# A two-layer hybrid decoder trunk: a recurrence without reciprocals, an output projection prepared in steps, value products of a pair in one go, and a compressed branch on the whole array

## The chip, the core and the metric

The kernel runs on one core of one Trainium2 chip. The time is what the device takes for one execution, in microseconds (us). Five engines have a part in it, each with its own instruction queue: TensorE (PE, with its weight loads PEld), VectorE (DVE), ScalarE (ACT), GpSimd (POOL) and SyncE (SP), which only starts transfers here. [...]

## The reference

Input is `x` (1024 rows of width 1024) and a memory of 256 rows. There are two layers. Each normalizes, projects once, runs three token mixers side by side, multiplies each with its own SiLU gate, and projects the joined result back with a residual sum.

Layer 0 mixes by sliding-window attention (A, 8 heads, window 128), by a gated linear recurrence (B, width 512), and by attention into the memory (M, 4 heads):

```python
# B, the recurrence
r = sigmoid(xh @ w_r + b_r); i = sigmoid(xh @ w_i + b_i)
log_a = -B_C * r * softplus(-lam)
a = exp(log_a)
u = sqrt(-expm1(2.0 * log_a)) * (i * xc)
h_t = a_t * h_(t-1) + u_t
...
return h + concatenate([oa, ob, om]) @ w_out
```

Layer 1 mixes by a chunked gated recurrence (C), by sparse attention (D, 8 heads in 2 groups) and again by attention into the memory. D has three branches, each with its own gate: a compressed one, which attends to 63 compressed keys of 64 numbers a group; a selected one, which attends to the chosen blocks; and a window of 512:

```python
p_c = softmax(where(mask_c, q @ kc * scale, NEG_INF))   # 63 compressed keys
o_cmp = p_c @ vc
...
o = g[..., 0, :] * o_cmp + g[..., 1, :] * o_sel + g[..., 2, :] * o_win
```

## The kernel before, in words

Projections are made of three matmuls each, of a high and a low part in place of f32 (`mm3`, L393 to L398): high by high, high by low, low by high. Scores are two such matmuls (L476, L477). Transposes (L256) and value products (L1436, L666, L813, L1364) are plain f32, of which a transpose is one instruction on PE and a product two.

The program is traced as generators. A main one goes through attention tiles of 128 rows; `weave` adds side generators to it. A side is written as (generator, n, y0, y1): its n steps are spread over the main steps y0 to y1. The order of each engine's queue comes from a scheduler at compile time, which takes the traced order as priority, holds each named ring of tiles to its count (the `B_` constants: `B_TR` for the transpose banks `tr`, `B_PT` for the transposed probabilities `PT`, `B_PS` for the probability tiles `Pt`, `B_HW` for the half-width tiles), and lets an instruction that is ready go ahead of one that isn't. Each engine then runs its queue in that order.

**Layer 0** has 24 tiles (8 of each attention group, then 8 of the memory attention) in a pipeline of 52 main steps: project, turn, probabilities, values. Beside them runs `side`, 24 steps from main step 0 to `E0`: gates and four blocks of the recurrence (`rglru_block`, L872), each in two halves of 128 x 512. A half makes a convolution on DVE (L890), two matmuls with tanh (L895, L896), a third tanh (L897), a square root (L899), a reciprocal (L902), products on POOL (L903, L904), the scan (L907) and the product with the gate (L508), and is stored to DRAM by `keep` (L540).

The output projection of layer 0 for rows 0 to 511 is `out_proj`, 16 steps from main step `E1` to `E2`. Its inputs are ten pieces of 128 x 512: eight come back from DRAM (`mixin`, L1469), two are the memory attention's, still in SBUF. `mix_parts` splits each into a high part on ACT (L1472) and a low part on DVE (L1473). A load must wait for a marker, `self.near`: a one-element copy on POOL (L1468) from a query tile of the memory attention, written where `s % 4 == NR` (L633). Called without a list `hl`, `out_proj` runs all of `mix_parts` in its first step. With a list it uses what another side has made; layer 1 did so already (L959).

**Layer 1** runs `nsa` twice, once a group, 8 tiles each. A tile has eight units, two for each pair: the window branch (`b` = 1) and the selected branch (`b` = 0), each with two pairs of heads. The first unit of a pair scores one head (`scored(0)`); `front` scores the other, takes the exponents (L1412) and scales (L1416). What is left of a pair is put on a list `late`, from which each unit takes one item as soon as more than two are on it. Before, a pair leaves two items, the first and the second half of its key tiles, in twos: each item transposes its tiles (`turned`, a copy out of PSUM by ACT, L1428) and multiplies them (`times`, L1436), where two heads fill the two halves of the array's columns. All branches of a tile add up in the one bank `ov`. `coarse` (L1353) begins that sum with the compressed branch: four transposes of 128 x 63, one copy (L1362), and two products of 64 columns by 256 (L1364).

Of the kernel before, what the change touches and what calls it, by code (L numbers as in the profile page):

```python
# [5 lines left out]
F32 = mybir.dt.float32  # L6
# [3 lines left out]
AF = mybir.ActivationFunctionType  # L10
# [4 lines left out]
P = 128  # L15
# [35 lines left out]
E0 = 38  # L51
# [13 lines left out]
B_TR = 4  # L65
B_OV = 1
NV = 4
N_LC0 = 1274
N_LC1 = 2428
B_PC = 3  # L70
N_FIX = 2966
NR = 2
# [9 lines left out]
def weave(main, *sides):  # L82
    drain(woven(main, *sides))
# [66 lines left out]
class Trunk:  # L150
# [108 lines left out]
    def setup(self):  # L259
        nc, I, const = self.nc, self.I, self.fixed  # L260
        self.ident = const.tile([P, P], F32, name="ident")
        nc.sync.dma_start(self.ident, I["c_ident"])
        rows = self.gt("rows", [P])
        for i, x in enumerate(("mem_norm_g", "norm_g")):
            nc.sync.dma_start(rows[16 * i:16 * i + 16, :], I[x].rearrange("l (k p) -> (l k) p", p=P))
        pt = self.tr()
        self.transpose(pt[:, 0, 0:32], rows[0:32, :], 32)
        self.gains = const.tile([P, 32], F32, name="gains")
        nc.vector.tensor_copy(self.gains, pt[:, 0, 0:32])
        self.mhalf = const.tile([P, 1], F32, name="mhalf")  # L270
# [235 lines left out]
    def mixmul(self, dst, o):  # L506

        self.nc.vector.scalar_tensor_tensor(out=dst, in0=o, scalar=0.5, in1=dst, op0=ALU.mult, op1=ALU.mult)  # L508
# [177 lines left out]
    def layer0(self):  # L686
# [73 lines left out]
        weave(pipe(tiles), (self.side, 24, 0, E0), (self.out_proj(0, I["ev_w_out"][0], 0, I["x"][0], self.h1), 16, E1, E2))  # L760
# [61 lines left out]
    def rglru_setup(self):  # L822
# [32 lines left out]
        nc.vector.scalar_tensor_tensor(out=sp2, in0=acc, scalar=4.0, in1=nl, op0=ALU.mult, op1=ALU.add)  # L855
        tiny = self.lc.tile([P, 1], F32, name="tiny")
# [7 lines left out]
        return prm, hb, sp2, tiny, bd  # L864
# [7 lines left out]
    def rglru_block(self, blk, b, prm, hb, sp2, tiny, bd, m):  # L872
# [3 lines left out]
        for half in range(2):  # L876
# [16 lines left out]
            for i, dst in enumerate((tr_, ti)):  # L893
                ps = self.sc()
                nc.tensor.matmul(ps, bd[:, i, b, :], xc, start=True, stop=True)  # L895
                nc.scalar.activation(dst, ps, AF.Tanh, scale=0.5, bias=hb[:, 4 * i + b:4 * i + b + 1])  # L896
            nc.scalar.activation(tr_, tr_, AF.Tanh, scale=sp2[:, b:b + 1], bias=sp2[:, b:b + 1])  # L897
            nc.vector.scalar_tensor_tensor(out=ti, in0=ti, scalar=1.0, in1=xc, op0=ALU.add, op1=ALU.mult)
            nc.scalar.activation(xc, tr_, AF.Sqrt, bias=tiny)  # L899
            nc.vector.tensor_scalar(out=tr_, in0=tr_, scalar1=1.0, scalar2=None, op0=ALU.add)  # L900
            inv = self.hw("inv", [H])
            nc.vector.reciprocal(inv, tr_)  # L902
            nc.gpsimd.tensor_tensor(out=xc, in0=xc, in1=inv, op=ALU.mult)  # L903
            nc.gpsimd.tensor_tensor(out=ti, in0=ti, in1=xc, op=ALU.mult)  # L904
            nc.vector.tensor_scalar(out=inv, in0=inv, scalar1=2.0, scalar2=-1.0, op0=ALU.mult, op1=ALU.add)
# [5 lines left out]
            self.mixmul(m[:, half, :], tr_)  # L911
# [300 lines left out]
    def compress(self, w):  # L1212
# [6 lines left out]
        vc = lc.tile([64, 2, HD], F32, name="vc")  # L1219
        kcT = lc.tile([P, 2, 64], F32, name="kcT")  # L1220
        self.cmp = (kcT, vc)
        for kind in range(2):
# [36 lines left out]
            hid = self.w1("hid", [2, 64])  # L1259
# [8 lines left out]
            nc.vector.scalar_tensor_tensor(out=hid[:, :, :NC], in0=th, scalar=1.0, in1=z, op0=ALU.add, op1=ALU.mult)  # L1268
            zc = self.sc()[0:NC, 0:P].rearrange("p (g d) -> p g d", g=2)
            for g in range(2):  # L1270
                nc.tensor.matmul(zc[:, g, :], hid[:, g, :NC], w2, start=True, stop=True)
            if kind == 1:
                nc.vector.tensor_copy(vc[0:NC], zc)
                yield
                continue
            n3 = lambda name: self.w1(name, [2, HD])[0:NC]
# [21 lines left out]
    def nsa_tile(self, blk, s, g, mixD):  # L1298
# [54 lines left out]
        def coarse():  # L1353
# [4 lines left out]
            pt = self.tr()  # L1358
            for h in range(4):
                self.transpose(pt[0:NC, h, :], pc[:, h, :NC])  # L1360
            PT = self.w2("PT", [4, P])
            nc.scalar.copy(PT[0:NC], pt[0:NC])  # L1362
            for f in range(2):
                nc.tensor.matmul(ov[f * HD:(f + 1) * HD, :], vc[0:NC, g, :], PT[0:NC].rearrange("p (h f) q -> p f h q", f=2)[:, f],  # L1364
                                 start=True, stop=False)

        def pair(b, hp):
# [72 lines left out]
            cut = (len(q0s) + 1) // 2  # L1440

            def back(part):
                for q0 in part:
                    turned(q0)
                for q0 in part:
                    times(q0)
                if part is q1 and b == 0 and hp == 1:
                    self.finish(1, 4 + 4 * g, s, mixD, st["ov"])

            q1 = q0s[cut:]  # L1450
            return [(lambda: scored(0), []), (front, [lambda: back(q0s[:cut]), lambda: back(q1)])]
# [126 lines left out]
```

## Time and profile before

| | |
|---|---|
| median of 3 runs | 1484.0 us (1481.54 to 1485.84) |
| the profiled execution: time, span | 1481.0 us, 1479.2 us |
| PE busy, instructions | 1406.0 us (95%), 10051 |
| DVE, ACT, POOL busy | 865.2, 657.6, 709.6 us |
| mean granted clock of PE | 0.982 |
| transfers | 108.54 MB, mean 73 GB/s |

Busy time is the share of the span in which an engine has at least one instruction under way; since matmuls are pipelined, a mean time of one matmul is longer than the distance to the next, so the text takes starts. The first projection of layer 1 follows the last output projection of layer 0 at 547 us. In rows of groups the columns are line, engine, operation, output from inputs, shapes and count, then busy time and mean ns of one, then the engine's idle time just before them and what ended it.

### The profile page before, as it was taken

How to read it: one execution, taken by the hardware profiler on the slowest of the kernel's cores; microseconds unless marked ns; L12 is line 12 of the kernel's file. 1: busy time of each engine (PE TensorE's matmuls, PEld its weight loads, DVE VectorE, ACT ScalarE, POOL GpSimd, SP SyncE). 2: the span in 40 equal slices, each digit the busy share in tenths (PEclk: the TensorE clock that was granted, in tenths of full speed). 3: DMA queues.
4: the chain of work that ended last, by engine and by line, in shares of the span. 5: the costliest groups of instructions: out<-in, count | busy, mean ns of one | idle time of the engine just before them, and what ended most of it. 6: DMA issues, size and time to landing. Idle time of an engine off the chain costs nothing.

```text
span 1479.2 us, 27613 instructions
## 1 busy us (share of the span) xinstructions
PE 1406.0 (95%) x10051; PEld 1222.1 (83%) x10051; DVE 865.2 (58%) x2497; ACT 657.6 (44%) x1636; POOL 709.6 (48%) x1125
## 2 busy tenths in 40 slices
PE   7999999999599999999999999999999988899999
PEld 6888888788489989898777777799988876788898
DVE  6667986866873428325565565445684567555621
ACT  7545654545553424124444454423342345455531
POOL 6344675564753334126544544335673557354521
PEclk9999999999899999999999999999999999899999
DMA  9420121122355554310000100031121001223323
GB/s 291 129 65 1 58 72 43 42 66 72 99 166 178 183 155 115 98 32 16 15 23 25 56 1 22 16 86 29 30 65 30 8 17 63 81 76 108 115 63 125
DMA packets 120619, 108.54 MB, mean 73 GB/s; under 512 B 19194, under 2 KB 108835, under 8 KB 120483
## 3 DMA queue, kind: packets, MB, share of 16 engines
q1 hardware_dynamic: 119906, 104.68, 23.6%
q0 software_dynamic: 576, 2.10, 0.5%
q8 instruction: 79, 1.29, 0.4%
q14 instruction: 58, 0.47, 0.1%
HBM read 87.35 MB, written 18.35 MB: 71 GB/s over the span
## 4 chain that ended last, share of the span: by engine, by line
PE 80%; DVE 8%; POOL 4%; ACT 3%; issue 3%; DMA 2%; SPq 1%; ACTq 0%; DVEq 0%; POOLq 0%
PE pj L396 17%; PE pj L397 17%; PE pj L398 17%; PE tr L256 8%; PE ov L1436 5%; PE sc L476 3%; PE sc L477 3%; DVE Pt L480 2%; PE sc L1067 1%; PE ov L813 1%; PE ov L666 1%; PE sc L398 1%; DMA mixin<-mix 1%; PE sc L396 1%; PE sc L397 1%
## 5 line engine op out<-in xcount | busy, mean ns | idle before, releaser
L398 PE MATMUL pj<-xn,whl 128*128 128x512 f32 x520 | 206.5, 397 | 0.0
L396 PE MATMUL pj<-xn,whl 128*128 128x512 f32 x520 | 206.3, 397 | 0.0
L397 PE MATMUL pj<-xn,whl 128*128 128x512 f32 x520 | 206.0, 396 | 0.0
L396 PE MATMUL pj<-whl,xn 128*128 128x256 f32 (+1 forms) x680 | 197.0, 293 | 3.6 <-ACT whl L247 3.0
L247 ACT CAST whl<-raw 128x512 fp32r<-128x512 f32 (+1 forms) x212 | 127.6, 614 | 162.6 <-PE pj L398 96.8
L397 PE MATMUL pj<-whl,xn 128*128 128x256 f32 (+1 forms) x680 | 197.4, 291 | 0.3 <-POOL whl L253 0.3
L398 PE MATMUL pj<-whl,xn 128*128 128x256 f32 (+1 forms) x680 | 196.3, 290 | 0.0
L396 PE MATMUL pj<-whl,mhi 128*128 128x256 f32 x640 | 184.1, 290 | 9.8 <-ACT mhi L1472 6.9
L253 POOL TENSOR_TENSOR whl<-raw,whl 128x512 fp32r<-128x512 f32 (+1 forms) x99 | 130.6, 1320 | 124.7 <-ACT whl L247 118.0
L397 PE MATMUL pj<-whl,mhi 128*128 128x256 f32 x640 | 182.8, 288 | 0.0
L398 PE MATMUL pj<-whl,mlo 128*128 128x256 f32 x640 | 179.8, 287 | 0.0
L1416 POOL TENSOR_SCALAR Pt<-Pt,fixed,lc 128x640 f32<-128x640 f32 (+7 forms) x128 | 107.0, 846 | 88.6 <-DVE fixed L1413 72.6
L396 PEld LDWEIGHTS pj<-whl,xn 128*128 128x128 f32 x680 | 129.9, 192 | 8.7 <-ACT whl L247 3.5
L397 PEld LDWEIGHTS pj<-whl,xn 128*128 128x128 f32 x680 | 131.0, 193 | 4.1 <-issue 1.9
L396 PEld LDWEIGHTS pj<-whl,mhi 128*128 128x128 f32 x640 | 123.3, 193 | 12.8 <-ACT mhi L1472 7.8
L253 DVE TENSOR_TENSOR whl<-raw,whl 128x512 fp32r<-128x512 f32 (+1 forms) x113 | 93.7, 832 | 68.0 <-ACT whl L247 67.7
L398 PEld LDWEIGHTS pj<-whl,xn 128*128 128x128 f32 x680 | 130.8, 193 | 1.7 <-issue 1.4
L256 PE MATMUL tr<-fixed,Pt 128*128 128x128 f32 x776 | 127.2, 286 | 5.3 <-DVE fixed L480 0.9
L1428 ACT COPY PT<-tr 128x512 f32<-128x512 f32 (+1 forms) x152 | 75.5, 530 | 114.1 <-PE tr L256 113.2
L1412 ACT ACTIVATE Pt<-Pt,fixed 128x640 f32<-128x640 f32 (+7 forms) x128 | 99.0, 776 | 60.0 <-DVE fixed L1409 32.3
L397 PEld LDWEIGHTS pj<-whl,mhi 128*128 128x128 f32 x640 | 123.9, 194 | 1.3 <-issue 1.2
L398 PEld LDWEIGHTS pj<-whl,mlo 128*128 128x128 f32 x640 | 122.2, 193 | 1.5 <-issue 1.4
(309 smaller groups left out, 3287.7 us busy)
## 6 DMA issues: line engine op xcount, KB each, us to landing
raw<-od_w_in SPq DMA_DIRECT2D x60, 256.0 KB, 3.9
raw<-ev_w_in SPq DMA_DIRECT2D x44, 256.0 KB, 4.4
raw<-ev_w_out SPq DMA_DIRECT2D x40, 256.0 KB, 4.0
raw<-od_w_out SPq DMA_DIRECT2D x40, 256.0 KB, 3.9
mixin<-mix SPq DMA_DIRECT2D x32, 256.0 KB, 3.6
raw<-mem_w_kv SPq DMA_DIRECT2D x16, 256.0 KB, 4.7
x<-x SPq DMA_DIRECT2D x8, 512.0 KB, 6.5
mix<-mix SPq DMA_DIRECT2D x8, 512.0 KB, 3.1
```

Source lines behind the costliest of these rows:

```text
L247: nc.scalar.copy(hi, src)
L253: eng.tensor_tensor(out=lo, in0=src, in1=hi.bitcast(F32), op=ALU.subtract)
L256: self.nc.tensor.transpose(out=out, in_=in_, identity=self.ident[0:np_, 0:np_])
L396: mm(ps, a[0], b[0], start=first, stop=False)
L397: mm(ps, a[0], b[1], start=False, stop=False)
L398: mm(ps, a[1], b[0], start=False, stop=last)
L476: mm(ps, qT[:, 0, h, :], kS, start=True, stop=False)
L477: mm(ps, qT[:, 1, h, :], kS, start=False, stop=last)
L1412: nc.scalar.activation(u["Pt"][e][:, :n], u["Pt"][e][:, :n], AF.Exp, bias=nm[:, e:e + 1], accum_out=den[:, e:e + 1], **scale)
L1416: nc.gpsimd.tensor_scalar(out=Pt[:, :n], in0=Pt[:, :n], scalar1=rd[:, e:e + 1], scalar2=gate(2 * hp + e, 1 + b), op0=ALU.mult, op1=ALU.mult)
L1428: nc.scalar.copy(PT[:, :2 * len(grp)], pt[:, :2 * len(grp)])
L1436: nc.tensor.matmul(st["ov"][f * HD:(f + 1) * HD, hp * P:(hp + 1) * P], vD[:, kt, b, :], PT[:, 2 * i + f, :], start=False, stop=b == 0 and ...
```

## The change

The recurrence gets `a` from an exponent: Exp gives a first value of `a`, a tensor_scalar makes (1 + a)/2 of it, which is a first value of the reciprocal of 1 plus the third tanh, and two scalar_tensor_tensor make one Newton step from it, negated; the product with the gate takes the sign out again. `mix_parts` of layer 0 becomes a side of its own, six steps from main step 39 to 45; `E0` goes from 38 to 36 and `NR` from 2 to 0. The two late items of a pair become one with all transposes and one with all products. In `coarse` two heads are transposed together (64 columns each, the 64th zero), and `vc` is kept as a block-diagonal 128 x 128 tile for each group, so that one product does both heads. `compress` writes its hidden values twice and makes 128 rows from them. `B_TR` goes from 4 to 3.

```diff
-E0 = 38
+E0 = 36
+MP = (39, 45)
...
-B_TR = 4
+B_TR = 3
...
-NR = 2
+NR = 0
...
+        for _ in range(B_PC):
+            nc.gpsimd.memset(self.w1("pc", [256]), 0.0)
...
-    def mixmul(self, dst, o):
+    def mixmul(self, dst, o, scale=0.5):
...
-        weave(pipe(tiles), (self.side, 24, 0, E0), (self.out_proj(0, I["ev_w_out"][0], 0, I["x"][0], self.h1), 16, E1, E2))
+        hl = []
+        weave(pipe(tiles), (self.side, 24, 0, E0), (self.mix_parts(0, I["ev_w_out"][0], 0, hl), 6, *MP),
+              (self.out_proj(0, I["ev_w_out"][0], 0, I["x"][0], self.h1, hl), 16, E1, E2))
...
+        nsp = self.lc.tile([P, 4], F32, name="nsp")
+        ts(out=nsp, in0=sp2, scalar1=-2.0, scalar2=None, op0=ALU.mult)
...
+            inv = self.hw("inv", [H])
+            nc.scalar.activation(inv, tr_, AF.Exp, scale=nsp[:, b:b + 1], bias=nsp[:, b:b + 1])
             nc.scalar.activation(tr_, tr_, AF.Tanh, scale=sp2[:, b:b + 1], bias=sp2[:, b:b + 1])
             nc.vector.scalar_tensor_tensor(out=ti, in0=ti, scalar=1.0, in1=xc, op0=ALU.add, op1=ALU.mult)
             nc.scalar.activation(xc, tr_, AF.Sqrt, bias=tiny)
-            nc.vector.tensor_scalar(out=tr_, in0=tr_, scalar1=1.0, scalar2=None, op0=ALU.add)
-            inv = self.hw("inv", [H])
-            nc.vector.reciprocal(inv, tr_)
-            nc.gpsimd.tensor_tensor(out=xc, in0=xc, in1=inv, op=ALU.mult)
+            nc.vector.tensor_scalar(out=inv, in0=inv, scalar1=0.5, scalar2=0.5, op0=ALU.mult, op1=ALU.add)
+            nc.vector.scalar_tensor_tensor(out=tr_, in0=tr_, scalar=1.0, in1=inv, op0=ALU.add, op1=ALU.mult)
+            nc.vector.scalar_tensor_tensor(out=inv, in0=tr_, scalar=-2.0, in1=inv, op0=ALU.add, op1=ALU.mult)
             nc.gpsimd.tensor_tensor(out=ti, in0=ti, in1=xc, op=ALU.mult)
-            nc.vector.tensor_scalar(out=inv, in0=inv, scalar1=2.0, scalar2=-1.0, op0=ALU.mult, op1=ALU.add)
+            nc.gpsimd.tensor_tensor(out=ti, in0=ti, in1=inv, op=ALU.mult)
+            nc.vector.tensor_scalar(out=inv, in0=inv, scalar1=-2.0, scalar2=-1.0, op0=ALU.mult, op1=ALU.add)
...
-        vc = lc.tile([64, 2, HD], F32, name="vc")
+        vc = lc.tile([P, 2, P], F32, name="vc")
+        nc.gpsimd.memset(vc, 0.0)
...
+            for a in range(2):
+                nc.vector.scalar_tensor_tensor(out=hid[:, :, a, :NC], in0=th, scalar=1.0, in1=z, op0=ALU.add, op1=ALU.mult)
+                nc.gpsimd.memset(hid[:, :, a, NC:], 0.0)
...
-            pt = self.tr()
-            for h in range(4):
-                self.transpose(pt[0:NC, h, :], pc[:, h, :NC])
-            PT = self.w2("PT", [4, P])
-            nc.scalar.copy(PT[0:NC], pt[0:NC])
-            for f in range(2):
-                nc.tensor.matmul(ov[f * HD:(f + 1) * HD, :], vc[0:NC, g, :], PT[0:NC].rearrange("p (h f) q -> p f h q", f=2)[:, f],
-                                 start=True, stop=False)
+            pt = self.pairs(pc.rearrange("p h n -> p (h n)"), 2)
+            PT = self.w2("PT", [2, P])
+            nc.scalar.copy(PT, pt)
+            nc.tensor.matmul(ov, vc[:, g, :], PT, start=True, stop=False)
...
-            def back(part):
-                for q0 in part:
+            def turns():
+                for q0 in q0s:
                     turned(q0)
-                for q0 in part:
+            def products():
+                for q0 in q0s:
                     times(q0)
...
-            return [(lambda: scored(0), []), (front, [lambda: back(q0s[:cut]), lambda: back(q1)])]
+            return [(lambda: scored(0), []), (front, [turns, products])]
```

More of the change, by code (lines that the diff above doesn't have):

```diff
@@ L64 @@
 B_SC = 4
-B_TR = 4
+B_TR = 3
 B_OV = 1
 NV = 4
-N_LC0 = 1274
-N_LC1 = 2428
+N_LC0 = 1278
+N_LC1 = 2556
 B_PC = 3
 N_FIX = 2966
-NR = 2
+NR = 0
 DEPTH = 2
@@ L504, in gate @@
         self.nc.vector.scalar_tensor_tensor(out=dst, in0=th, scalar=1.0, in1=z, op0=ALU.add, op1=ALU.mult)
-    def mixmul(self, dst, o):
-        self.nc.vector.scalar_tensor_tensor(out=dst, in0=o, scalar=0.5, in1=dst, op0=ALU.mult, op1=ALU.mult)
+    def mixmul(self, dst, o, scale=0.5):
+        self.nc.vector.scalar_tensor_tensor(out=dst, in0=o, scalar=scale, in1=dst, op0=ALU.mult, op1=ALU.mult)
     def gates(self, w, off, m, by_half=False):
@@ L863, in rglru_setup @@
                 nc.sync.dma_start(bd[c * HD:(c + 1) * HD, i, :, c * HD:(c + 1) * HD], ap[c])
-        return prm, hb, sp2, tiny, bd
+        return prm, hb, sp2, nsp, tiny, bd
     def rglru(self, w, b, prm):
@@ L870, in rglru, with rglru_block @@
         yield from self.rglru_block(blk, b, *prm, m)
-    def rglru_block(self, blk, b, prm, hb, sp2, tiny, bd, m):
+    def rglru_block(self, blk, b, prm, hb, sp2, nsp, tiny, bd, m):
         nc = self.nc
@@ L910, in rglru_block @@
                 nc.gpsimd.tensor_copy(last, tr_[:, H - 1:H])
-            self.mixmul(m[:, half, :], tr_)
+            self.mixmul(m[:, half, :], tr_, -0.5)
             self.keep(0, 4 + b, half, m[:, half:half + 1, :])
@@ L1258, in compress @@
             nc.vector.tensor_scalar(out=pb[:, 1:2], in0=pb[:, 0:1], scalar1=0.5, scalar2=None, op0=ALU.mult)
-            hid = self.w1("hid", [2, 64])
+            hid = self.turn("hid", 1, 256, "hid", [4, 64]).rearrange("p (g a) n -> p g a n", g=2)
             ps = self.sc()[:, 0:2 * NC].rearrange("p (g n) -> p g n", g=2)
@@ L1267, in compress @@
             nc.vector.tensor_scalar(out=z, in0=ps, scalar1=pb[:, 0:1], scalar2=0.5, op0=ALU.add, op1=ALU.mult)
-            nc.vector.scalar_tensor_tensor(out=hid[:, :, :NC], in0=th, scalar=1.0, in1=z, op0=ALU.add, op1=ALU.mult)
-            zc = self.sc()[0:NC, 0:P].rearrange("p (g d) -> p g d", g=2)
+            for a in range(2):
+                nc.vector.scalar_tensor_tensor(out=hid[:, :, a, :NC], in0=th, scalar=1.0, in1=z, op0=ALU.add, op1=ALU.mult)
+                nc.gpsimd.memset(hid[:, :, a, NC:], 0.0)
+            zc = self.sc()[:, 0:P].rearrange("p (g d) -> p g d", g=2)
             for g in range(2):
-                nc.tensor.matmul(zc[:, g, :], hid[:, g, :NC], w2, start=True, stop=True)
+                nc.tensor.matmul(zc[:, g, :], hid[:, g].rearrange("p a n -> p (a n)"), w2, start=True, stop=True)
             if kind == 1:
-                nc.vector.tensor_copy(vc[0:NC], zc)
+                for a in range(2):
+                    nc.vector.tensor_copy(vc[a * HD:(a + 1) * HD, :, a * HD:(a + 1) * HD], zc[a * HD:(a + 1) * HD])
                 yield
                 continue
+            zc = zc[0:NC]
             n3 = lambda name: self.w1(name, [2, HD])[0:NC]
@@ L1439, in pair @@
             q0s = list(range(0, len(kts), 2))
-            cut = (len(q0s) + 1) // 2
-            def back(part):
-                for q0 in part:
+            def turns():
+                for q0 in q0s:
                     turned(q0)
-                for q0 in part:
+            def products():
+                for q0 in q0s:
                     times(q0)
-                if part is q1 and b == 0 and hp == 1:
+                if b == 0 and hp == 1:
                     self.finish(1, 4 + 4 * g, s, mixD, st["ov"])
-            q1 = q0s[cut:]
-            return [(lambda: scored(0), []), (front, [lambda: back(q0s[:cut]), lambda: back(q1)])]
+            return [(lambda: scored(0), []), (front, [turns, products])]
         units = [x for b in (1, 0) for hp in range(2) for x in pair(b, hp)]
```

## The prediction

> **What bounds the kernel now.** I read the page first, for the shares and the slices.
>
> ```profile
> PE 1406.0 (95%) x10051; PEld 1222.1 (83%) x10051; DVE 865.2 (58%) x2497; ACT 657.6 (44%) x1636; POOL 709.6 (48%) x1125
> ...
> PE   7999999999599999999999999999999988899999
> ...
> PE 80%; DVE 8%; POOL 4%; ACT 3%; issue 3%; DMA 2%; SPq 1%; ACTq 0%; DVEq 0%; POOLq 0%
> ```
>
> PE is busy 95% of the span and carries 80% of the chain that ended last, so time leaves this kernel in two ways only: PE gets less work where it is full, or a hole of PE is filled. The slices show one deep hole (the 5, eleventh digit) and a shallow one (8s from the 33rd). I then asked for stretches around them; the columns are start and end, length, then busy time of PE, PEld, DVE, ACT and POOL with instruction counts, the granted clock, DMA share and GB/s.
>
> ```profile
> 350.00:420.00 70.00, 50.74 (x389) 44.50 (x388) 58.43 (x129) 42.34 (x100) 45.53 (x70) 0.93 0.38 122
> 420.00:545.00 125.00, 124.59 (x1058) 122.25 (x1057) 50.41 (x104) 44.77 (x97) 44.38 (x66) 1.00 0.54 165
> 600.00:1200.00 600.00, 583.09 (x4092) 493.77 (x4090) 327.67 (x1114) 231.57 (x626) 279.15 (x471) 0.99 0.13 34
> 1200.00:1300.00 100.00, 84.96 (x630) 69.63 (x628) 64.22 (x209) 49.04 (x120) 54.07 (x92) 0.90 0.21 68
> ```
>
> In 350 to 420 PE stands idle for 70.00 - 50.74 = 19.3 us and loses clock besides (0.93); in 1200 to 1300 it is idle 15.0 us, in the 600 us before that 16.9 us. The timeline of PE names what ended the idle time of the first hole (start, length, instruction, and in brackets the idle time before it and its releaser):
>
> ```profile
> 377.30 3.75 PE L895 MATMUL sc<-xc,bd 128*128 128x512 f32 x4 [7.61 <-DVE xc L890]
> 385.85 1.09 PE L666 MATMUL ov<-PT,vm 128*64 128x128 f32 x16 [2.45 <-ACT PT L241]
> 388.53 0.38 PE L476 MATMUL sc<-mkS,qT 128*128 128x256 f32 x1 [0.93 <-POOL qT L471]
> 391.66 0.44 PE L396 MATMUL pj<-whl,mhi 128*128 128x256 f32 x1 [2.39 <-ACT mhi L1472]
> 399.90 0.39 PE L396 MATMUL pj<-whl,mhi 128*128 128x256 f32 x1 [3.15 <-ACT mhi L1472]
> 417.21 0.39 PE L396 MATMUL pj<-whl,mhi 128*128 128x256 f32 x1 [2.72 <-DVE fixed L1502]
> ```
>
> The projections of layer 0 are used up; left are the last recurrence block (L890, L895), the memory tiles (L666), and the first output projection, whose split inputs (mhi) are not there: a supply hole, and DVE is busy 58.43 of its 70 us.
>
> **The recurrence without reciprocals.** Out go L900, L902 and L905; in come one tensor_scalar, two scalar_tensor_tensor and one tensor_scalar on DVE, and an Exp on ACT. POOL keeps two products.
>
> ```profile
> L902 DVE RECIPROCAL inv<-tr 128x512 f32<-128x512 f32 x8 | 26.8, 3344 | 0.1
> L905 DVE TENSOR_SCALAR inv<-inv 128x512 f32<-128x512 f32 x8 | 6.8, 849 | 0.0
> L898 DVE SCALAR_TENSOR_TENSOR ti<-ti,xc 128x512 f32<-128x512 f32 x8 | 5.9, 742 | 3.0 <-ACT ti L896 3.0
> L900 DVE TENSOR_SCALAR tr<-tr 128x512 f32<-128x512 f32 x8 | 4.2, 529 | 3.1 <-ACT xc L899 3.1
> L897 ACT ACTIVATE tr<-tr,lc 128x512 f32<-128x512 f32 x8 | 6.5, 814 | 0.2
> ```
>
> Per half block DVE loses 3344 + 529 + 849 = 4722 ns and gains 529 + 2 x 742 + 849 = 2862 ns: 1.86 us less, 14.9 us over the eight. ACT gains 814 ns by the row of its neighbour. The new DVE steps need only the Exp and the Tanh, not the Sqrt, so the reciprocal leaves the latency of a block too. Until about 350 us PE is full and this is worth nothing; in the hole two of the eight reciprocals (366.7 and 387.6 us by DVE's timeline) stand in front of the memory tiles' work. The Exp comes from the same engine as the Tanh, and its cover is ACT's 40% idle time there (42.34 of 70); uncovered it would cost 0.8 us a half.
>
> ```profile
> 366.69 3.34 DVE L902 RECIPROCAL inv<-tr 128x512 f32<-128x512 f32 x1
> ...
> 372.87 0.41 DVE L508 SCALAR_TENSOR_TENSOR mix<-ov,mix 128x256 f32<-128x256 f32 x1
> ...
> 387.15 0.42 DVE L508 SCALAR_TENSOR_TENSOR mix<-ov,mix 128x256 f32<-128x256 f32 x1
> 387.56 3.35 DVE L902 RECIPROCAL inv<-tr 128x512 f32<-128x512 f32 x1
> ...
> 402.62 0.42 DVE L508 SCALAR_TENSOR_TENSOR mix<-ov,mix 128x256 f32<-128x256 f32 x1
> ...
> 408.54 0.42 DVE L508 SCALAR_TENSOR_TENSOR mix<-ov,mix 128x256 f32<-128x256 f32 x1
> ```
>
> These L508 rows end memory tiles 0 to 3. They come 14.3, 15.5 and 5.9 us apart: the pace is 6 us once the recurrence is out of the way.
>
> **The first output projection in steps.** Before, all of mix_parts is issued in the first step of out_proj, at main step 47: eight loads on SP, ten casts on ACT, ten subtractions on DVE, five weight chunks. Now they come one part a step from 40 to 45, the marker NR lets the loads go after memory tile 0 or 4 instead of 6, and E0 ends the recurrence two of 52 steps earlier. On SP the loads pass weight and residual loads that were ahead of them; the one that could block SP is the last recurrence block's part, which must first be stored, but that block ends by step 36. On POOL eight one-element copies move, too small to count. On DVE and ACT the splits now fall into the hole's front, where DVE is the fuller, but the 3.7 us that the last block saves there pays for part of them. When memory tile 3 is done the projection is ready. Upper bound: all 19.3 us of idle, and the clock's 0.07 x 70 = 4.9 us. Lower bound: 0, as nothing is taken away that PE needs. I take two thirds of the idle, 13 us, and none of the clock: tiles 3 to 7 are a chain of their own, and only three projection banks can be filled ahead of the last part. Late next: the memory tiles.
>
> **Value products of a pair in one go.** The two halves of a pair's second stage (transpose some, multiply some, twice) become all transposes, then, a unit later, all products. A burst of products has a price at its two ends, seen by the starts of what follows:
>
> ```profile
> 1389.99 0.28 PE L476 MATMUL sc<-kS,qT 128*128 128x256 f32 x1
> 1390.11 0.28 PE L477 MATMUL sc<-kS,qT 128*128 128x256 f32 x1
> 1390.32 0.66 PE L1436 MATMUL ov<-PT,vD 128*64 128x128 f32 x8
> 1390.91 0.66 PE L256 MATMUL tr<-fixed,Pt 128*128 128x128 f32 x4
> 1391.50 0.44 PE L1436 MATMUL ov<-PT,vD 128*64 128x128 f32 x4
> 1391.87 0.66 PE L256 MATMUL tr<-fixed,Pt 128*128 128x128 f32 x4
> ```
>
> Four products take 0.37 us to the next start, eight 0.59: 0.055 us each and 0.15 fixed. The start into a burst is 0.21 us after the instruction before it, where 0.12 is usual: 0.09 more. So a burst less saves 0.24 us. The code makes two bursts of each pair with three or more key tiles, 6 of 8 tiles, for two branches, two pairs and two groups: 48 pairs. 48 x 0.24 = 11.5 us of PE. Bounds: 0 if the compile-time scheduler goes on mixing them, and more if it now splits even single halves.
>
> The order also frees the probability tiles (four, two to a pair) a unit earlier, and lets the copies land before they are needed:
>
> ```profile
> DVE Pt L480 <- PE tr L256: 34.0, 28, 4.6
> PE ov L1436 <- ACT PT L1428: 6.4, 9, 2.3
> L1428 ACT COPY PT<-tr 128x512 f32<-128x512 f32 x112 | 61.9, 586 | 88.6 <-PE tr L256 88.2
> ```
>
> The first row (us in total, times, longest) is DVE waiting for transposes to give up a tile; the second is PE waiting for a copy. Against it stands B_TR, four transpose banks to three. A group of four transposes needs about 0.44 us (eight take 0.87, next fence), its copy 0.586, so four groups in a row run at the copy's pace unless other matmuls stand between. I take 4 us gained, between 10 lost and 15 gained (the idle of 1200 to 1300).
>
> **Compressed branch on the whole array.** Per tile four transposes become two, and four half-wide products of 256 columns become two whole ones (each f32 product is two instructions).
>
> ```profile
> 1395.36 0.28 PE L397 MATMUL pj<-whl,mhi 128*128 128x256 f32 x1
> 1395.56 0.65 PE L1364 MATMUL ov<-PT,lc 63*64 63x256 f32 x4
> 1396.14 1.09 PE L1436 MATMUL ov<-PT,vD 128*64 128x128 f32 x16
> ...
> 1056.07 1.03 PE L256 MATMUL tr<-fixed,Pt 128*128 128x128 f32 x8
> 1056.94 0.38 PE L256 MATMUL tr<-fixed 128*128 128x128 f32 x2
> ...
> 643.11 3.28 PE L1262 MATMUL sc<-U,w 128*128 128x126 f32 x28
> 646.15 0.36 PE L396 MATMUL pj<-whl,xn 128*128 128x256 f32 x1
> ```
>
> Old: 0.58 us to the next start and 0.08 more on entry, 0.66. New: a whole-array f32 pass of 126 columns takes 3.04 / 28 = 0.109 us, so 256 take 0.22, two 0.44, without the ends. Saved 0.22, and two transposes at 0.87 / 8 = 0.109: 0.44 a tile, 7.0 us over 16. [...] The added memsets (three of the ring at the start, vc, hid) run on POOL while PE waits for its first loads or is fed by others; uncovered, some 2 us.
>
> **Sum.** The profiled execution took 1481.0 us around a span of 1479.2; the median of three is 1484.0, 3.0 above it. PE's own saving is 11.5 + 7.0 = 18.5 us; all of it lies in layer 1, where some stretches are not full of PE, so I count three quarters, 14. With 13 for the hole and 4 for waits: 31 less, 1450 against the profiled execution, 1453 as a median.
>
> **The rivals.** (1) The hole stays: the memory tiles, not the splits, set it. For it: two of six idle times end on L666 and L476. Then only layer 1 gains, 1484 - 18 = 1466. (2) The scheduler goes on issuing products group by group as copies land: 11.5 x 0.75 = 9 us less gain, 1462. (3) The other side: three transpose banks make PE wait on ACT's copies. There are 112 full copies (the row above); it decides once each costs PE 31 / 112 = 0.28 us more than now, and at 0.37 the time is 1453 + 41 = 1494. Against it: 88 us of waiting stands with ACT, for PE, and not the reverse. (4) No change: a new order of all queues opens as many holes as it closes, 1484.
>
> **How the numbers follow.** Forecast 0.47, the hole staying 0.20, products split 0.16, no change 0.07, three banks 0.10. A measurement tells about 0.3%, 4.5 us: faster is the first three, 0.83. The range goes down to 1433 (all of the hole with its clock, 11 more, and 9 of the holes in layer 1) and up to 1475, past both partial cases; about 0.2 lies outside.
>
> **What would show it.** Right: no reciprocal of 128x512 on DVE, PE idle under 8 us around 350 to 420, products in runs of 20 to 32 with some 65 to 80 runs, one wide product a tile, L480's wait on transposes near nothing. Wrong: idle before the mhi matmuls as large as now, or new idle time of PE with ACT's PT copy as releaser.

## The result, and the profile after

The changed kernel takes 1465.3 us (median of 4 runs, 1462.0 to 1467.9) against 1482.8 us for the kernel before in the same series: a ratio of 0.988 (0.985 to 0.991), 17.5 us less. The forecast was 1453, the range 1433 to 1475. A second series of the changed kernel gave 1465.0 us and 0.9885 (0.9865 to 0.9904). The profile of after is of a run of 1467.9 us with a span of 1466.1. Line numbers are a few higher than before (L396 is now L400, L480 L484, L1436 L1450, L666 L670).

From the page, as before: engines, slices of PE, the chain.

```profile
PE 1395.5 (95%) x9987; PEld 1221.9 (83%) x9987; DVE 854.1 (58%) x2509; ACT 661.4 (45%) x1644; POOL 705.9 (48%) x1133
...
PE   7899999999889999999999989999999987999999
...
PE 84%; DVE 5%; DMA 3%; POOL 3%; ACT 2%; issue 2%; SPq 1%; DVEq 0%; ACTq 0%; POOLq 0%
```

PE has 64 instructions less and is as full as before. The deep hole (the 5) has become two 8s. The same stretches as before (length, busy time of PE, PEld, DVE, ACT, POOL, then the granted clock):

```profile
350.00:420.00 70.00, 58.48 (x451) 50.76 (x450) 56.99 (x139) 47.36 (x111) 49.49 (x77) 0.95 0.40 129
420.00:545.00 125.00, 122.65 (x1038) 121.06 (x1037) 47.18 (x97) 43.51 (x92) 43.88 (x65) 1.00 0.54 165
600.00:1200.00 600.00, 581.51 (x4094) 498.81 (x4093) 337.03 (x1142) 233.15 (x638) 283.18 (x484) 0.99 0.13 34
1200.00:1300.00 100.00, 84.98 (x649) 70.18 (x649) 63.55 (x208) 49.69 (x125) 52.21 (x86) 0.93 0.24 78
```

Idle time of 350 to 420 fell from 19.3 to 11.5 us, not under 8; the hole of 1200 to 1300 is as wide as it was (15.0 us). The new recurrence is there (view of single lines: count, shortest, median and longest ns, first and last start), and so is the wide product:

```profile
L908 ACT ACTIVATE inv<-tr,lc x8: 803/806/812, 141.0 to 366.0; 128x512 f32<-128x512 f32 x8
L913 DVE SCALAR_TENSOR_TENSOR tr<-tr,inv x8: 680/692/1805, 145.5 to 370.1; 128x512 f32<-128x512 f32 x8
L914 DVE SCALAR_TENSOR_TENSOR inv<-tr,inv x8: 674/686/1669, 148.4 to 373.5; 128x512 f32<-128x512 f32 x8
L1379 PE MATMUL ov<-PT,lc x32: 377/379/415, 680.9 to 1380.6; 128*128 128x256 f32 x32
```

The waits that the pair order was to take away:

```profile
DVE Pt L484 <- PE tr L257: 23.3, 14, 3.4
PE ov L1450 <- ACT PT L1442: 2.4, 5, 0.8
PE tr L257 <- ACT PT L1442: 1.9, 4, 0.8
```

DVE's wait fell from 34.0 to 23.3 us, PE's for copies from 6.4 to 2.4. The third row was this before:

```profile
PE tr L256 <- ACT PT L1428: 0.8, 1, 0.8
```

It is 0.8 us as well in no_pairs and recurrence_three_banks, two of the kernels below, which have three banks and a pair's two halves as before. So the 1.1 us more come with the pair order on three banks, not with three banks by themselves.

All runs are set side by side in one table. Its times between marks are taken from the starts of matmuls on PE: **start** is the first matmul to the first attention product (L813 before), **layer 0** from there to the first compressed score, **group 1** on to the last product but one of the 528 of the first group, **between** to the first of the last 528, **group 2** to the last of those; 50.4 us of projection follow in every kernel. **Runs** counts uninterrupted runs of value products (L1436 before) in the trace. **Idle** is PE's idle time between its first and last matmul, **half** the time in that stretch in which the profile records a granted clock of 0.50. What is left of the stretch, after idle time and half of the half-clock time are taken off, I call PE's **own work**; that split is an estimate.

| kernel | ratio to before (interval) | runs | start | layer 0 | group 1 | between | group 2 | idle | half | own work |
|---|---|---|---|---|---|---|---|---|---|---|
| before | 1 | 122 | 129.9 | 527.3 | 300.5 | 190.5 | 271.0 | 63.7 | 55 | 1378 |
| after | 0.988 (0.985 to 0.991) | 109 | 135.8 | 518.7 | 291.9 | 189.8 | 269.3 | 60.6 | 55 | 1368 |
| after_again | 0.9885 (0.9865 to 0.9904) | 109 | 134.5 | 517.9 | 292.0 | 189.8 | 267.2 | 62.1 | 38 | 1371 |
| no_recurrence | 0.9909 (0.9891 to 0.9926) | 109 | 135.3 | 523.4 | 292.3 | 189.8 | 269.7 | 62.9 | 61 | 1367 |
| no_steps | 0.9924 (0.9907 to 0.9941) | 108 | 133.7 | 511.4 | 303.3 | 189.8 | 268.1 | 60.4 | 55 | 1369 |
| no_pairs | 0.9981 (0.9967 to 0.9994) | 136 | 133.8 | 517.2 | 300.8 | 189.0 | 272.4 | 61.7 | 44 | 1380 |
| narrow_branch | 0.9934 (0.9915 to 0.9952) | 113 | 134.0 | 521.3 | 294.8 | 190.2 | 274.6 | 55.2 | 72 | 1374 |
| recurrence_alone | 0.9865 (0.9841 to 0.9889) | 122 | 130.2 | 512.7 | 301.6 | 190.4 | 263.9 | 50.1 | 31 | 1384 |
| recurrence_three_banks | 0.9965 (0.9950 to 0.9980) | 131 | 135.6 | 513.1 | 303.2 | 187.2 | 276.1 | 56.1 | 48 | 1386 |
| ring_five | 0.9981 (0.9965 to 0.9996) | 110 | 132.8 | 519.0 | 302.4 | 189.8 | 271.7 | 66.7 | 55 | 1372 |
| reverse_order | 0.9947 (0.9928 to 0.9965) | 72 | 135.4 | 521.2 | 303.3 | 186.7 | 269.7 | 73.6 | 68 | 1359 |
| reverse_first | 0.9911 (0.9892 to 0.9931) | 63 | 134.3 | 520.5 | 297.5 | 186.8 | 264.2 | 69.8 | 48 | 1360 |
| reverse_first_six | 0.9969 (0.9957 to 0.9981) | 63 | 137.0 | 522.1 | 298.9 | 190.5 | 270.9 | 72.1 | 92 | 1352 |
| reverse_no_steps | 0.9901 (0.9880 to 0.9922) | 62 | 134.9 | 510.4 | 300.6 | 189.0 | 270.6 | 68.8 | 65 | 1355 |

How far one profile is from another of the same kernel is seen in the second and third row: spans of 1466.1 and 1461.9 us, and 17 us less at half clock. Differences of a few us in the last three columns mean nothing alone; ratios are medians with intervals, and 0.001 is 1.5 us. One run of ring_five (2703 us) and one of reverse_order (4131 us) lie far outside all others and are left out of the ratios.

### The profile page after: what moved, and what is told of

Read it like the earlier page. It is cut to its first block, busy times and chain, and to the rows that moved or that the text cites. A ratio compares the mean times of both kernels' runs of the same rounds, so it can differ in the third digit from the quotient of the medians.

```text
span 1466.1 us, 27523 instructions
## 1 busy us (share of the span) xinstructions
PE 1395.5 (95%) x9987; PEld 1221.9 (83%) x9987; DVE 854.1 (58%) x2509; ACT 661.4 (45%) x1644; POOL 705.9 (48%) x1133
## 4 chain that ended last, share of the span: by engine, by line
PE 84%; DVE 5%; DMA 3%; POOL 3%; ACT 2%; issue 2%; SPq 1%; DVEq 0%; ACTq 0%; POOLq 0%
PE pj L400 18%; PE pj L402 18%; PE pj L401 18%; PE tr L257 8%; PE ov L1450 5%; PE sc L480 3%; PE sc L481 3%; PE sc L1079 1%; DVE Pt L484 1%; PE ov L670 1%; PE ov L819 1%; DMA x<-x 1%; PE sc L1339 1%; PE sc L903 1%; DMA raw<-mem_w_kv 1%
## 5 line engine op out<-in xcount | busy, mean ns | idle before, releaser
L400 PE MATMUL pj<-xn,whl 128*128 128x512 f32 x520 | 207.8, 400 | 0.0
L400 PE MATMUL pj<-whl,xn 128*128 128x256 f32 (+1 forms) x680 | 196.7, 293 | 4.7 <-ACT whl L248 3.2
L400 PE MATMUL pj<-whl,mhi 128*128 128x256 f32 x640 | 182.6, 288 | 7.6 <-ACT mhi L1486 5.2
L1430 POOL TENSOR_SCALAR Pt<-Pt,fixed,lc 128x640 f32<-128x640 f32 (+7 forms) x128 | 103.0, 812 | 87.3 <-DVE fixed L1427 60.9
L400 PEld LDWEIGHTS pj<-whl,xn 128*128 128x128 f32 x680 | 130.2, 193 | 9.3 <-ACT whl L248 3.8
L257 PE MATMUL tr<-fixed,Pt 128*128 128x128 f32 x776 | 124.1, 282 | 13.0 <-POOL Pt L1430 3.6
L400 PEld LDWEIGHTS pj<-whl,mhi 128*128 128x128 f32 x640 | 123.1, 193 | 10.6 <-ACT mhi L1486 6.7
L254 DVE TENSOR_TENSOR whl<-raw,whl 128x512 fp32r<-128x512 f32 (+1 forms) x113 | 90.7, 806 | 63.5 <-ACT whl L248 63.3
```

What stands on the lines that cost most here:

```text
L254: eng.tensor_tensor(out=lo, in0=src, in1=hi.bitcast(F32), op=ALU.subtract)
L257: self.nc.tensor.transpose(out=out, in_=in_, identity=self.ident[0:np_, 0:np_])
L400: mm(ps, a[0], b[0], start=first, stop=False)
L1430: nc.gpsimd.tensor_scalar(out=Pt[:, :n], in0=Pt[:, :n], scalar1=rd[:, e:e + 1], scalar2=gate(2 * hp + e, 1 + b), op0=ALU.mult, op1=ALU.mult)
```

## The experiments: one part undone

The first four ran together: the changed kernel again, and three kernels with one part of the change undone.

**after_again**, no edit. 

> The changed kernel once more, five rounds, so that the kernels with a part taken out again have it beside them on the same chip. Expected 1462 to 1468 us and a ratio to the kernel before of 0.985 to 0.991 by its four runs so far. Its first profile had TensorE at half clock for 13.6 us in the first 50 us and 6 us more spent before the first value product of layer 0; if that is chance, this profile has it not; if it comes from the three transpose banks, it is here again.

Measured 1465.0 us, 0.9885. The result stands. The late start is here again, with 134.5 us to the first attention product and 10.2 us at half clock in the first 50 us, so it isn't chance.

**no_recurrence**: reciprocals as before.

```diff
-            nc.scalar.activation(inv, tr_, AF.Exp, scale=nsp[:, b:b + 1], bias=nsp[:, b:b + 1])
...
+            nc.vector.reciprocal(inv, tr_)
+            nc.gpsimd.tensor_tensor(out=xc, in0=xc, in1=inv, op=ALU.mult)
```

> The changed kernel with the recurrence as before (reciprocal of 128x512 on VectorE, eight times). Theory: reciprocals matter only where TensorE has run out of projections, after 350 us, and there are two: 2 to 4 us slower than the changed kernel. Rival: 15 us of VectorE work count wherever memory or attention tiles wait for VectorE, so 8 to 12 us slower. Second rival: nothing, since the hole is set by the memory tiles: within 1 us.

Measured 0.9909: 3.6 us more than after by the ratios, 4.8 by the medians (1469.8 against 1465.0); layer 0 takes 5.5 us more. The theory's 2 to 4 us held as closely as the intervals tell. By itself this reads as "the recurrence is worth 4 us"; the run of the recurrence alone, below, gives another price.

**no_steps**: `out_proj` makes all parts in its first step, `E0` 38, `NR` 2.

```diff
-E0 = 36
-MP = (39, 45)
+E0 = 38
-NR = 0
+NR = 2
-        weave(pipe(tiles), (self.side, 24, 0, E0), (self.mix_parts(0, I["ev_w_out"][0], 0, hl), 6, *MP),
-              (self.out_proj(0, I["ev_w_out"][0], 0, I["x"][0], self.h1, hl), 16, E1, E2))
+        weave(pipe(tiles), (self.side, 24, 0, E0), (self.out_proj(0, I["ev_w_out"][0], 0, I["x"][0], self.h1), 16, E1, E2))
```

> The changed kernel with the first output projection of layer 0 as before (E0 38, NR 2, all of mix_parts in its first step). Theory: the split inputs were what TensorE lacked; the idle time of 350 to 420 us goes from 11.5 us back to some 17, and the kernel is 6 to 9 us slower than the changed one. Rival: the recurrence's shorter chain filled the hole and the steps add nothing: within 1.5 us.

Measured 0.9924, 5.8 us more by medians: the theory's size, and not its place. Layer 0, the only part of the program that the edit touches, became 6.5 us shorter (511.4 against 517.9). The loss is in group 1, 11.3 us longer, hundreds of us later. Set against each other in the traces, PE's 5672 instructions from the first value product on are in another order from the 282nd on, and 528 places hold another instruction: the scheduler, given another layer 0, ordered layer 1 otherwise. In group 1 the profile has 5.1 us more idle time than after_again and 10.3 us more at half clock, worth 5.1, which is nearly all of the loss. So my reading of the hole falls with this run although its number came out.

**no_pairs**: two late items a pair, as before.

```diff
-            return [(lambda: scored(0), []), (front, [turns, products])]
+            return [(lambda: scored(0), []), (front, [lambda: back(q0s[:cut]), lambda: back(q1)])]
```

> The changed kernel with the two halves of a pair as before (transpose some, multiply some, twice). The compiled order has 134 runs of value products in place of 107. Theory: a run's ends cost 0.24 us, so 27 x 0.24 = 6.5 us of TensorE, and some waits on top: 7 to 9 us slower than the changed kernel. Rival: the ends of a run hide (in the first profile of the changed kernel 13 runs fewer took only 1.4 us off these products), and the first group's 8.5 us came from elsewhere: 1 to 3 us slower.

Measured 0.9981: 14 us slower than after by the ratios (0.0096 x 1483, give or take 3.5), twice the theory. There are 136 runs of products for 109, as expected 27; PE's own work is 9 to 12 us larger, of which 27 x 0.24 = 6.5 by the price of the forecast. Laid to the runs alone it would be 0.33 to 0.44 us a run; whether the rest belongs to them is open, and I can't lay it to one wait.

## The price of a run's ends

Was the price of 0.24 us a run wrong, or the count? The next kernels issue a pair's products from the last group of key tiles to the first, so that the first product waits for the last copy and nothing splits the rest. Both are built with one buffer less in the 512-wide ring, so that alone was run as their base.

**ring_five**: `B_HW` 5 for 6. 

> The changed kernel with one buffer less in the ring of 512-wide work tiles (B_HW 5 for 6), nothing else. It is the base for the two kernels that follow, which only fit in memory with five. Value products still stand in 109 runs in the issued order. Theory (the ring is not short): within 2 us of the changed kernel. Rival (layer 0 lacks the sixth tile): 3 to 8 us slower, all of it ahead of the first compressed score.

Measured 0.9981, 14 us slower than after (0.0096 again). Neither case held: layer 0, where a sixth tile could be missed, is as long as it was (519.0 against 517.9), and group 1 is 10.4 us longer. The trace shows one place of it, in group 1 (start, length, instruction, idle time and releaser), and then, as stretches, the clock around it:

```profile
821.19 0.55 PE L257 MATMUL tr<-fixed,Pt 128*128 128x128 f32 x3 [0.26 <-POOL Pt L1430]
824.03 1.12 PE L257 MATMUL tr<-fixed,Pt 128*128 128x128 f32 x4 [2.29 <-ACT PT L1442]
825.08 1.12 PE L1450 MATMUL ov<-PT,vD 128*64 128x128 f32 x8
```

```profile
821.00:824.00 3.00, 0.55 (x3) 0.31 (x3) 2.27 (x5) 2.72 (x6) 2.83 (x5) 1.00 0.00 0
824.00:827.40 3.40, 3.37 (x20) 2.38 (x22) 1.31 (x5) 0.96 (x2) 3.01 (x4) 0.50 0.00 0
827.40:831.00 3.60, 3.60 (x32) 3.05 (x28) 2.92 (x11) 2.14 (x5) 0.00 (x0) 1.00 0.32 77
```

Transposes wait 2.29 us for ACT to empty a bank, and then PE has a granted clock of 0.50 for 3.4 us: four transposes take 1.12 us where 0.66 was usual. In group 1 this kernel has 20.5 us at half clock and 17.0 us of idle time, the changed kernel 6.8 and 13.7: half of the one difference and all of the other are 10.1 us, the whole loss of group 1 in the profile. At the place shown this is rival 3's mechanism, in a kernel where it wasn't sought; why the order of layer 1 changed with a ring of layer 0 wasn't followed.

**reverse_order**:

```diff
-                for q0 in q0s:
+                for q0 in q0s[::-1]:
                     times(q0)
```

> Products of a pair issued from the last group of key tiles to the first, so that the first product waits for the last copy and the rest can follow in one run: 72 runs in the issued order for 109. Theory (a run's two ends cost PE 0.24 us and PE is the bound of layer 1): 37 x 0.24 = 8.9 us less than with five ring tiles, 6 to 9 after what does not lie on the path. Rival 1 (an end of a run is paid only where PE is not waiting anyway): within 2 us. Rival 2 (the last copy comes late, and PE stands before the first product): 3 to 10 us more, with the PT copy as PE's releaser for over 10 us in total (2.4 us in the changed kernel).

Measured 0.9947: 5.0 us less than ring_five (0.0034 x 1485, give or take 4). 72 runs for 110. PE's own work fell by 13 us, but idle time rose by 7 us and half-clock time by 14: in the profiles all of it was given back, by the medians more than half. The theory's 6 to 9 and rival 1's 2 are both within reach of the interval; rival 2's waits for copies (2.6 us for products) didn't come.

**reverse_first**: the same, with the products ranked ahead of other ready work (`with self.tc.high_priority():`). 

> The same reverse order, with the products ranked ahead of other work that is ready: 62 runs for 109. Theory: 47 x 0.24 = 11.3 us less than with five ring tiles, 8 to 11 on the path. Rival 1: within 2 us. Rival 2: slower than the reverse order alone by 2 us or more, with more idle time of PE before value products.

Measured 0.9911: 10.4 us less than ring_five (0.0070, give or take 0.0026), and PE's own work 12 us less. With 47 runs fewer that is 0.22 to 0.26 us a run, which agrees with the price in the forecast; the interval of the ratios alone allows 0.14 to 0.30. A run of eight in after, and one of 20 here:

```profile
1393.44 0.23 PE L1403 MATMUL sc<-lc,fixed 128*128 128x128 bf16 x1
1393.61 0.66 PE L1450 MATMUL ov<-PT,vD 128*64 128x128 f32 x8
1394.19 0.39 PE L400 MATMUL pj<-whl,mhi 128*128 128x256 f32 x1
```

```profile
1393.14 1.31 PE L1450 MATMUL ov<-PT,vD 128*64 128x128 f32 x20
1394.38 0.38 PE L401 MATMUL pj<-whl,mhi 128*128 128x256 f32 x1
```

Eight take 0.58 us to the next start, 20 take 1.24: 0.055 us for each one more, so 0.14 us at the end at both lengths.

**narrow_branch**: the changed kernel with the compressed branch as before.

```diff
-            nc.tensor.matmul(ov, vc[:, g, :], PT, start=True, stop=False)
+            for f in range(2):
+                nc.tensor.matmul(ov[f * HD:(f + 1) * HD, :], vc[0:NC, g, :], PT[0:NC].rearrange("p (h f) q -> p f h q", f=2)[:, f],
+                                 start=True, stop=False)
```

> The changed kernel with the compressed branch as before (four transposes and four half-wide products a tile, no added memsets). Value products in 110 runs. Theory (the wide branch is worth what PE's charged time fell by: products 9.3 to 7.0 us and two transposes a tile of 0.109 us, 3.5 us): 4 to 6 us more than the changed kernel. Rival (a wide product gains nothing over two half-wide ones that share the array): 2 to 4 us more, from the transposes alone. Second rival (a new order of the queues outweighs the part): outside 1 to 7 us either way.

Measured 0.9934, 7.3 us more than after (0.0049, give or take 0.0027). The first theory's 4 to 6 and a little more; the rival's 2 to 4 lies at the end of the interval. From start to next start, the 32 wide products take 7.0 us, where the 64 half-wide ones take 9.3 here and took 9.3 before; two transposes a tile at 0.109 add 3.5. So the wide branch is worth 5.8 us of PE, not 7.0, and two whole products take 0.44 us a tile where four half-wide ones take 0.58. By the run of 20 above, a half-wide product goes at 0.055 us for 128 columns, so four of 256 columns would be 0.44 too; the 0.14 us more is the price at the end of a run.

## One part alone, and the banks

**recurrence_alone**: the kernel before with the new recurrence, four banks, nothing else. 

> The kernel before with the new recurrence and nothing else (four transpose banks, 122 runs of value products as before). Without the steps, but with the rest, layer 0 took 511 us from the first attention product to the first compressed score, against 527 before and 518 with everything. Theory (the reciprocals made the hole, the steps add nothing): 10 to 16 us faster than before, 1468 to 1473, PE idle 8 to 13 us in 350 to 420. Rival (the hole needs the steps; the recurrence is worth the 4 to 5 us that its removal cost): 3 to 6 us faster. Second rival (the hole moves elsewhere, as POOL's longer chain comes late): within 2 us.

Measured 1462.9 us, 0.9865 (0.9841 to 0.9889). That is as fast as the whole change; the intervals overlap. It is 21 us faster than before, where the theory had 10 to 16. Layer 0 fell by 14.6 us, the theory's amount. Another 7 us came from group 2, where half-clock time fell from 20.5 to 6.8 us though in the traces the order on PE from the first value product on is that of before in 5437 of 5732 places; how much of those 7 is the order and how much one profile against another, I can't say.

```profile
350.00:420.00 70.00, 63.40 (x512) 57.66 (x511) 61.76 (x136) 44.77 (x103) 51.80 (x74) 0.95 0.48 149
1200.00:1300.00 100.00, 91.01 (x734) 74.74 (x734) 66.68 (x230) 58.62 (x145) 57.16 (x94) 0.97 0.25 77
```

PE's idle time of 350 to 420 is 6.6 us here and 11.5 with all parts. Why the steps make it worse is seen on DVE, in the rows that end attention tiles and memory tiles, here and in after. First the last attention tile, memory tile 0 and memory tile 7 of recurrence_alone:

```profile
345.55 0.42 DVE L508 SCALAR_TENSOR_TENSOR mix<-ov,mix 128x256 f32<-128x256 f32 x1 [1.04 <-PE ov L813]
358.40 0.41 DVE L508 SCALAR_TENSOR_TENSOR mix<-ov,mix 128x256 f32<-128x256 f32 x1
...
441.72 0.42 DVE L508 SCALAR_TENSOR_TENSOR mix<-ov,mix 128x256 f32<-128x256 f32 x1 [3.54 <-PE ov L666]
```

The same three in after:

```profile
362.41 0.39 DVE L512 SCALAR_TENSOR_TENSOR mix<-ov,mix 128x256 f32<-128x256 f32 x1
377.30 0.42 DVE L512 SCALAR_TENSOR_TENSOR mix<-ov,mix 128x256 f32<-128x256 f32 x1
...
455.54 0.42 DVE L512 SCALAR_TENSOR_TENSOR mix<-ov,mix 128x256 f32<-128x256 f32 x1 [3.46 <-PE ov L670]
```

Counted from the first attention product (135.3 and 142.2 us), the last attention tile ends at 210 us in the one and 220 in the other, memory tile 0 at 223 and 235, tile 7 at 306 and 313. The steps did what they say: by the same count the first matmul of a split input starts at 236 us with them and at 244 without. But the attention of layer 0 ends 10 us later with them, before any split is made (the first at 230 us), and everything behind it is late. That the other parts of the change aren't the reason is seen in no_steps, which differs from the changed kernel by the steps alone: there the same three are at 211, 224 and 308 us. Over all profiles layer 0 takes 510 to 513 us without the steps and with the new recurrence (four kernels), 517 to 522 with both (seven kernels), 523 with the steps and the old recurrence, 527 before. So the steps cost 6 to 12 us where the recurrence is fast (no_steps against after_again, and the last pair below); where it is slow, layer 0 is 4 us shorter with them and the other parts (no_recurrence against before). Which of their three parts costs it, the recurrence's earlier end (`E0` 36), the early loads (`NR`) or the splits, wasn't run; that the attention is already late points to `E0`, and so does that the recurrence ends 8 us earlier with the steps (its last half at 242 us, against 250 in no_steps). It stays open.

**recurrence_three_banks**: `B_TR` 3 for 4 beside it. 

> The same with three transpose banks for four (130 runs of value products for 122). Theory (every kernel with three banks reached its first attention product 3 to 6 us later than the kernel before, and more runs cost 8 x 0.24 = 1.9 us): 4 to 8 us slower than the recurrence alone, 3 to 6 of it ahead of that product. Rival (the start comes late for the other edits, the memsets on POOL among them): within 2 us, and the start as before.

Measured 0.9965: 15 us slower than with four banks (0.0100, give or take 0.0028), twice the theory. 5.4 us of it lie ahead of the first attention product, as every kernel with three banks shows (133 to 137 us, against 130 with four). With four banks:

```profile
0.00:100.00 100.00, 89.14 (x611) 82.44 (x612) 66.73 (x160) 61.69 (x146) 46.61 (x87) 1.00 0.52 163
25.00:50.00 25.00, 21.55 (x177) 20.73 (x176) 18.72 (x42) 15.39 (x35) 15.24 (x23) 1.00 0.79 249
```

With three:

```profile
0.00:100.00 100.00, 85.31 (x572) 79.04 (x573) 63.07 (x150) 59.08 (x138) 41.26 (x83) 0.97 0.47 156
25.00:50.00 25.00, 21.53 (x160) 21.09 (x159) 17.10 (x37) 14.94 (x35) 10.45 (x15) 0.86 0.68 215
```

In the first 100 us PE gets 39 matmuls less done: in the traces PE's order differs from the 14th matmul on, among the transposes of the inputs. The other large difference is group 2, 12.2 us longer, with 5.4 us more idle time and 13.7 us more at half clock, worth 6.8. Part of that is the short group 2 in the profile of the recurrence alone: against before it is 5.1 us longer. What in three banks opens these holes wasn't followed. The rival, that the start is late for the memsets, falls: this kernel has none of them.

The last two try all that looked good together. They have six 512-wide tiles, the reversed products ranked first, and one buffer less in the ring of small 256-wide tiles, which makes room. With the shorter ring a small tile is written again while a later step still needs it, so part of the values that they compute differ from the reference's; number and shape of the instructions are as described, and their times stand for that alone.

**reverse_first_six**: with the steps. 

> The changed kernel with all six ring tiles, products in reverse order and ranked first (63 runs for 109), which fits with one buffer less in the ring of small 256-wide tiles (B_W1 6 for 7). Theory (46 run ends less at 0.24 us): 11 us less than the changed kernel, ratio to the kernel before 0.980 to 0.983. Rival (the 10 us that the kernel with five ring tiles lost between the first and the 527th value product come back with any new order of the queues): 0.986 to 0.992.

Measured 0.9969. The theory's 0.980 to 0.983 fell, and it is slower than the rival's upper end too. PE's own work is the smallest of all, 16 us below after, but idle time (72.1 us) is among the largest and half-clock time (92 us) is the largest. The stretch that was 0.90 of the clock before:

```profile
1200.00:1300.00 100.00, 80.32 (x570) 67.85 (x568) 61.36 (x198) 48.26 (x125) 53.09 (x91) 0.86 0.20 64
```

**reverse_no_steps**: without them. 

> The same without the steps (first projection's parts in one go, E0 38, NR 2; 62 runs). Theory (layer 0 is 5 to 7 us shorter without the steps): 5 to 7 us less than with them, ratio 0.976 to 0.979. Rival (the order of layer 1 changes with it, as it did when the steps were taken out of the changed kernel): no gain or a loss of up to 6 us against the kernel with steps.

Measured 0.9901: 10 us less than with the steps (0.0068, give or take 0.0024), more than the theory's 5 to 7; layer 0 alone is 11.7 us shorter. So the steps cost in this pair too; the ratio of 0.976 to 0.979 was missed because the kernel with the steps was so much slower than expected. Neither kernel beats the changed one: the fastest measured are the whole change and the recurrence alone, which these runs can't tell apart.

## Why the forecast came out as it did

The sum said 31 us less, and 17.5 came; the time lies in the range, 12 us above the value and nearer to rivals 1 (1466) and 2 (1462). Of its terms one was near, one came out in part but for another reason than the one given, and two failed. That the time still fell into the range is partly luck.

**The hole, 13 us.** Layer 0 became 9 us shorter in the profiles, 7 of them idle time (23.9 to 16.8 us): near two thirds of the term. The step that failed is who fills it. I put the gain down to the split inputs ("when memory tile 3 is done the projection is ready") and gave the recurrence only part of the cost of the splits as pay. The runs showed the reverse: the recurrence alone takes 14.6 us off layer 0, and the steps give 6 or more of them back. The line "late next: the memory tiles" and rival 1 named what holds PE then; I hadn't seen that the attention before them comes late as well. That I took none of the clock was wrong by a little: half-clock time in layer 0 went from 20.5 to 13.7 us, worth 3.

**Bursts of products, 11.5 us, counted at three quarters.** The price was right, 0.22 to 0.26 us measured against 0.24. The count was wrong: 48 runs less were forecast, 65 to 80 left, and there are 109 for 122. The code gives products one late item, but the scheduler lets what is ready go first, so it issues them group by group as copies land: this is rival 2, which I gave 0.16. The reverse order bears it out: there the first product waits for the last copy, and the runs fall to 72. Against the same kernel without the pair order it is 27 runs less; the missing 14 came with the other parts, three banks among them (9 in recurrence_three_banks). 13 x 0.24 = 3.1 us is what this term brought against before.

**Compressed branch, 7.0 us.** 5.8 us on PE, 7.3 by its removal. The two new passes take 0.22 us each from start to start, as forecast. By the rate alone the wide product gains nothing in this trace: 0.055 us for 128 columns of a half-wide product (the run of 20 in reverse_first) is half of the 0.109 of a whole-array transpose (0.87 us for eight, before). With the price at the end of a run it does: the half-wide products take 9.3 us against 7.0. The prediction set 0.66 against 0.44 without telling the two apart.

**Waits and three banks, 4 us gained, between 10 lost and 15 gained.** This is the step that failed most. The waits I had named did shrink, DVE's by 10.7 us and PE's for copies by 4.0 (less the 1.1 us by which the third row grew). But three banks cost 15 us beside the recurrence alone, more than the lower bound of the whole term, and mostly not by the mechanism of rival 3: PE waits for ACT's copies 6.7 us in that kernel, against 4.5 with four banks. The waits of recurrence_alone, then of recurrence_three_banks:

```profile
PE ov L1442 <- ACT PT L1434: 3.7, 8, 0.7
PE tr L256 <- ACT PT L1434: 0.8, 1, 0.8
```

```profile
PE ov L1442 <- ACT PT L1434: 5.9, 10, 1.1
PE tr L256 <- ACT PT L1434: 0.8, 1, 0.8
```

The start, 5.4 us of it, isn't in the forecast at all. I had costed the bank where value products use it, and not at its other users. The changed kernel with four banks wasn't run, so what the fourth bank is worth there stays open.

**The sum.** Undone one at a time the parts are worth 4 (recurrence), 6 (steps), 14 (pairs) and 7 us (compressed branch), by medians or ratios, 31 in all. Less the 15 us that three banks cost beside the recurrence that would be 16, near the 17.5 measured; but this adds figures of two different kernels, and no run shows that it holds. Other figures don't add: the recurrence alone is worth 21 (1462.9 against 1484.2 us), as much as all parts together, and its removal costs 4. A part removed from the whole and the same part added alone are two questions here: the removal also reorders queues that it doesn't touch.

## What to carry to other kernels

Price a shared resource at each of its users, the first 100 us of the program among them, before giving one of it away for a part that gains a few us. Where a scheduler orders the queues, count runs and waits in the order that it issues, not in the order of the code, and test a part alone as well as its removal: here one part alone was worth the whole change, and its removal showed a fifth of that. When work is taken from a full engine, look at idle time and granted clock in the same table, since both gave back here what the work had saved (reverse_order: 13 us less work, 7 more idle and 14 more at half clock).

## What was not expected of the hardware

A short stall of PE was followed by a loss of clock: in ring_five, in the place shown, a stall of 2.29 us and then 3.4 us at a granted clock of 0.50, by the split above (an estimate) another 1.7 us of work. Yet a stall of 1.97 us in the second profile of the changed kernel had none behind it. In the clock records the changes lie multiples of 3.41 us apart; in before and after the times at half clock between them are 3.41, 6.83 or 10.24 us long. So I cut all 14 profiles, from 20 us on, into stretches of 3.41 us between those changes, and counted how busy PE was in a stretch at full clock, and how often the next was at half clock. The last column has the same count for before and after alone:

| busy share of PE in the stretch | stretches | next at half clock | in before and after |
|---|---|---|---|
| under 0.40 | 85 | 85 | 9 of 9 |
| 0.40 to 0.50 | 56 | 40 | 6 of 8 |
| 0.50 to 0.60 | 70 | 20 | 3 of 11 |
| over 0.60 | 5496 | 1 | 0 of 788 |

These are counts from the traces of this case; what sets the clock isn't shown by them. The two stalls fit. The stretch ahead of the half clock in ring_five:

```profile
820.60:824.00 3.40, 0.85 (x4) 0.45 (x4) 2.67 (x6) 2.72 (x6) 3.23 (x5) 1.00 0.00 0
```

PE is busy 0.85 of 3.40 us, a quarter. The stall in after_again (PE's wait ends at 861.26 us) falls on two stretches:

```profile
857.22:860.63 3.41, 2.07 (x14) 1.86 (x12) 3.35 (x20) 3.27 (x13) 1.31 (x2) 1.00 0.03 5
860.63:864.04 3.41, 1.97 (x14) 1.74 (x15) 2.53 (x10) 1.29 (x3) 3.14 (x6) 1.00 0.01 2
```

PE is busy 0.61 and 0.58 of them; between 0.50 and 0.60, 50 of 70 stretches kept the clock, and over 0.60 all but one. The stall of 2.29 us lies in one stretch, that of 1.97 us across two: what a stall costs here depends on where it lies too, which moves with everything ahead of it. The changed kernel had 7 such losses of clock in one profile (after_again) and 10 in the other (after), the recurrence alone 6, reverse_first_six 14. For the way back, of 164 stretches at half clock in which PE was over 0.80 busy, 146 were followed by full clock, of the 50 below that none (18 of 22 and 0 of 8 in before and after).
